# Layer 1 of a two-layer decoder trunk: mean products a step behind their adds, output weights split ahead of convolution taps, a planner that counts more vector work

## The chip, the cores and the metric

The kernel runs on one core of one Trainium2 chip. The metric is the device time of one execution, in microseconds (us). TensorE (PE) multiplies matrices, VectorE (DVE), ScalarE (ACT) and GpSimd (POOL) do elementwise work, and SyncE (SP) issues the transfers. Each engine takes its instructions in the order in which the program lists them for it, and waits at an instruction until what it needs is there.

## The reference

Two residual layers over 2048 tokens of width 1024. Layer 0 (sparse attention beside a gated MLP) is not touched by the change. Layer 1 is a convolution module:

```python
def conv_layer(h, w_in, dw_w, dw_b, ln_g, ln_b, w_out):
    a, gl, z = jnp.split(h @ w_in, 3, axis=-1)
    y = a * jax.nn.sigmoid(gl)
    y = depthwise_causal_conv(y, dw_w, taps=31) + dw_b      # per channel
    y = jax.nn.silu(layer_norm(y, ln_g, ln_b))
    return (y * jax.nn.silu(z)) @ w_out

x = x + rms_norm(conv_layer(rms_norm(x, g_pre), ...), g_post)
```

(`depthwise_causal_conv` stands for the grouped convolution call of the original.)

## The kernel before, in words

Layer 1 works on the sequence in two halves of 1024 tokens. `layer1_in` multiplies the normalised input by the input weights on PE (L161 to L163: every product is three, of high and low parts) and leaves, per 128 channels, a gated tile `y` of 1024 tokens (evicted by DVE at L1007) or a gate `z`, which goes to memory.

The convolution has 31 taps per tile and is shared out by a planner that runs while the program is written. `conv_vector` issues a tap on DVE (L1134, accumulating into `acc`, which lies in PSUM in a pool named `psc` with two slots). `conv_pool` issues a tap as a product on ACT (L1100) and an add on POOL (L1101, into `cacc` in SBUF). DVE joins the two sums in one add (L1140, `cout`), which is stored to `yc_d` in memory. The planner keeps a clock for DVE (`"v"`) and one for POOL (`"p"`); `busy` adds the assumed length of an instruction, and `beat` advances the time by the length of one PE tile (5.12) and issues taps on each of the two until its clock has caught up. So assumed lengths decide how many taps go into the order between other work. `drain(half, k)` issues all taps that are left.

`gated_norm(c, hand)` is a generator of eight steps for a chunk c of 256 tokens (c = 0 to 7; 0 to 3 belong to the first half, 4 to 7 to the second). It loads the convolved chunk from `yc_d`; adds and folds it over channels (L1214, L1202, L1203 on DVE) and takes the mean by a product with a matrix of ones (L1207 on PE); subtracts (L1221), squares on ACT (L1223), adds on POOL (L1224), folds and takes the mean again (L1202, L1203, L1207); square root on ACT (L1233), reciprocal (L1234) and scaling (L1245) on DVE; silu on ACT (L1251), gate on POOL (L1253); and splits the result into high and low parts (L122 on ACT, L125 on POOL). The sum, its folds and the mean product stand in one step. `l(c, m)` advances chunk c to step m.

`wout_pieces` loads the output weights in four pieces of 128 x 4 x 512 into a raw slot and splits each (L122 on ACT, L125 on DVE). `out_project` then makes the output of 128 tokens, called a row tile t0, t1, ... here: 48 matmuls (L842 to L844) in two PSUM tiles, a sum of squares on ACT (L854), square root (L865) and reciprocal (L866), the eviction with the post-norm (L874, `yn`, on DVE), the residual add on POOL (L875) and the store. Chunk c gives t(2c) and t(2c+1).

`tail` holds the order. While the second half's input products run, the norms of c = 0 to 2 are advanced; then the output weights are split; then the loop over c issues the row tiles, with the norms of later chunks and the last taps between them. Before c = 2 the pool `psc` is closed and its PSUM is given to the row tiles, and `gated_norm(4)` starts with `drain(2, 0)`. The Tile framework schedules the written program once more, so the order that stands on each engine is shown below from the built program.

Of the kernel before, what the change touches and what calls it, by code (L numbers as in the profile page):

```python
# [10 lines left out]
F32 = mybir.dt.float32  # L11
# [8 lines left out]
P = 128  # L20
# [61 lines left out]
class Trunk:  # L82
# [723 lines left out]
    def wout_pieces(self, W, raws, places, which, w, lo):  # L806

        nc = self.nc
        w = w if w else {}
        for i in which:  # L810
            n, h = divmod(i, 2)
            w[n, h] = [self.tile(pool, [P, 4, 512], F32R, *tag) for pool, *tag in places[i]]
            pool, tag, *bufs = raws[i]
            raw = self.tile(pool, [P, 4, 512], F32, tag, *bufs)
            nc.sync.dma_start(raw, W[512 * h:512 * h + 512, 512 * n:512 * n + 512]
                              .rearrange("(k p) n -> p k n", p=P))
            self.split(*w[n, h], raw, nc.scalar, lo)
        return w

    def wout_early(self):  # L820
# [257 lines left out]
    def conv_pool(self):  # L1078


        nc = self.nc
        room = lambda c, n: c["end"] - c["tap"] > n
        q = [c for c in self.queue if room(c, 1)]
        if not q:
            q = [c for c in self.now if room(c, 1 if c["sum"] else 6)]
        if not q:
            return False
        c = q[0]
        c["end"] -= 1
        win, w = self.conv_args(c, c["end"])  # L1090
        if c["sum"] is None:
            c["sum"] = self.tile(self.cp, [P, HALF], F32, "cacc", 2)
            if c["bias"] is None:
                nc.scalar.activation(c["sum"], win, AF.Copy, scale=w)
            else:
                nc.scalar.activation(c["sum"], win, AF.Identity, scale=w, bias=c["bias"])
                c["bias"] = None
        else:
            t = self.tile(self.cp, [P, HALF], F32, "prod", 2)
            nc.scalar.activation(t, win, AF.Copy, scale=w)  # L1100
            nc.gpsimd.tensor_tensor(c["sum"], c["sum"], t, ALU.add)  # L1101
            self.busy("p", 2.4)
        return True

    def conv_args(self, c, j):
# [3 lines left out]
    def conv_vector(self):  # L1109

        nc, v = self.nc, self.nc.vector
        if len(self.now) < 2 and self.queue:
            self.now.append(self.queue.pop(0))
        if not self.now:
            return False
        c = self.now.pop(0)
        j = c["tap"]
        c["tap"] += 1
        win, w = self.conv_args(c, j)
        last = c["tap"] == c["end"]  # L1120
        old, acc = c["acc"], c["acc"]
        if last and not (acc and c["sum"]):
            acc = self.tile(self.cp, [P, HALF], F32, "cout", 1)
        elif acc is None:
            acc = self.tile(self.psc, [P, HALF], F32, "acc", 2)
        if old is None and (last or self.clock["p"] < self.clock["v"] + AHEAD):
            old, c["sum"] = c["sum"], None
        if old is None and c["bias"] is not None:
            v.tensor_scalar(acc, win, w, c["bias"], ALU.mult, ALU.add)
            c["bias"] = None  # L1130
        elif old is None:
            v.tensor_scalar(acc, win, w, None, ALU.mult)
        else:
            v.scalar_tensor_tensor(acc, win, w, old, ALU.mult, ALU.add)  # L1134
        c["acc"] = acc
        self.busy("v", 1.2 if self.now else 1.33)
        if last:
            if c["sum"]:
                acc = self.tile(self.cp, [P, HALF], F32, "cout", 1)
                v.tensor_tensor(acc, c["acc"], c["sum"], ALU.add)  # L1140
                self.busy("v", 1.33)
            r, s = P * c["k"], HALF * c["half"]
            nc.sync.dma_start(self.yc_d[r:r + P, s:s + HALF], acc)
        else:
            self.now.append(c)
        return True
# [28 lines left out]
    def gated_norm(self, c, hand):  # L1175

        nc, pool = self.nc, self.lp
        v = nc.vector
        b4 = lambda: self.tile(pool, [P, 4, 256], F32, "b4", 5)
# [25 lines left out]
        def mean(s):  # L1205
            o = self.tile(*self.pt)
            nc.tensor.matmul(o[:, :256], self.mean1, s[:, 0], start=True, stop=True)  # L1207
            return o[:, :256]
# [4 lines left out]
        s = tmp()  # L1213
        v.tensor_tensor(s, Y[0], Y[1], ALU.add)  # L1214
        fold(s)
        m = mean(s)
        self.busy("v", 2.1)
        yield
        sq = []
        for y in Y:  # L1220
            v.tensor_tensor(y, y, wide(m), ALU.subtract)  # L1221
# [4 lines left out]
        self.busy("p", 2.3)  # L1226
        yield
        fold(sq[0])
        var = mean(sq[0])
        self.busy("v", 0.9)  # L1230
        yield
        rs = self.tile(self.late_conv, [P, 256], F32, "lrs", 1)
        nc.scalar.activation(rs, var, AF.Sqrt, bias=self.eps)  # L1233
        v.reciprocal(rs, rs)  # L1234
# [13 lines left out]
        for q, (y, z) in enumerate(zip(Y, zs)):  # L1248
            for i in range(4):
                k = 4 * q + i  # L1250
# [5 lines left out]
        hi, lo = (self.tile(pool, [P, KT, 256], F32R, f"h{2 + 4 * (c % 2) + i}") for i in range(2))  # L1256
        for q, y in enumerate(Y):
            s = slice(4 * q, 4 * q + 4)
# [11 lines left out]
    def tail(self, w1):  # L1270

        with ExitStack() as ctx:
            self.gp = self.pool(ctx, "gpost")
            lp = self.lp = self.pool(ctx, "late")
# [14 lines left out]
            step = lambda g, n=1: [next(g, None) for _ in range(n)]  # L1289
# [14 lines left out]
            n = 8  # L1304
# [4 lines left out]
            def l(c, m):  # L1309
                while c < n and at[c] < m:  # L1310
                    next(ln[c])
                    at[c] += 1
# [4 lines left out]
            for i in range(1, 44):  # L1317
                step(z)
                for c in range(3):
                    l(c, min(7, i + 1 - c))  # L1320
            step(z)
            places = [[(lp, "whiA"), (lp, "wloA")], [(lp, "h0"), (lp, "h1")],
                      [(inner, "whiB"), (inner, "wloB")], [(lp, "h4"), (lp, "h5")]]
            wout = lambda which, w=None: self.wout_pieces(self.a["odd_w_out"][0], [(lp, "wraw")] * 3 + [(lp, "h6")], places, which, w, self.nc.vector)
            w = wout([0])
            step(z, 2)
            w = wout([1], w)
            gpost = self.load_gpost(1)
            l(0, 8)
            step(z, 3)  # L1330
            w = wout([2, 3], w)
            for c in range(n):
                t0, t1 = (self.out2(c, i, hand[c], w, gpost) for i in range(2))
                if c == 2:
                    self.pt = self.ps, [P, 512], F32, "A", 3
                    self.psx.close()
                    self.ps = self.pool(self.psx, "ps4", 4, PSUM)
                step(t0), self.beat()
                l(c + 1, 8), l(c + 2, 2)
                step((t0, t1)[c == 0]), self.beat()  # L1340
                l(c + 2, 3)
                step((t0, t0)[c == 0]), self.beat(5.12 if c == 0 else 0)
                step((t1, t0)[c == 0]), self.beat(5.12 if c else 0)
                l(c + 2, 5)
                step(t1), self.beat()
                l(c + 2, 7), l(c + 3, 1)
                step(t1)


    def run(self):  # L1350
# [60 lines left out]
```

## Time and profile before

| | |
|---|---|
| Time, median of 3 runs | 2279.05 us (2277.89 to 2279.7) |
| Profiled execution, its own time | 2275.86 us, of which span 2274.1 |
| PE busy | 2202.5 us, 97% of the span |
| DVE, ACT, POOL busy | 68%, 55%, 62% |

The profile follows one execution. A row of the stretches view gives, for a window, the busy time and the number of instructions of each engine and the granted clock of PE as a share of full speed (1.00 is 2.4 GHz, 0.50 is 1.2 GHz). A row of the waits view says for which instruction of another engine an engine stood idle, for how long in all, how often, and the longest. A row of the timeline gives start, length, engine, line and operation, and in brackets the idle time before it with what ended it.

### The profile page before, as it was taken

The page shows a single profiled execution, that of the slowest core. Times are in us where ns is not written, and L with a number is a line of the kernel's source. Part 1 is how long each engine was busy: PE and PEld are TensorE (multiplying, and loading weights), DVE is VectorE, ACT ScalarE, POOL GpSimd, SP SyncE. Part 2 cuts the span into 40 slices and gives each one's busy share as a digit, 9 for nine tenths or more (in the row PEclk, how much of TensorE's full clock was granted, in tenths as well). Part 3 has the DMA queues.
Part 4 walks back from the last instruction along what each step waited for, and adds up shares of the span by engine and source line. Part 5 has one row for each costly group of instructions (what it writes and reads, how often), then busy time and mean ns, then how long its engine had stood idle before and what let it go on. Part 6 is the DMA issues. An engine that isn't in the chain of part 4 may idle for free.

```text
span 2274.1 us, 34588 instructions
## 1 busy us (share of the span) xinstructions
PE 2202.5 (97%) x12414; PEld 1907.0 (84%) x12414; DVE 1547.0 (68%) x3272; ACT 1258.6 (55%) x2345; POOL 1400.6 (62%) x1351
## 2 busy tenths in 40 slices
PE   8999999999989999999999989999999989998998
PEld 7898889988878999898998978888888778886877
DVE  3441324365248998888889844527998899999772
ACT  5231232253258888878898854425555575556463
POOL 5232222243237778667789644548999579999683
PEclk9999999999999999999999999999999999999999
DMA  6252231442281111100113154651222432224641
GB/s 161 94 190 88 79 107 53 145 138 86 89 235 53 32 41 29 29 22 25 29 54 110 45 169 151 215 187 47 84 75 83 139 111 65 74 93 145 226 167 65
DMA packets 244860, 229.19 MB, mean 101 GB/s; under 512 B 33841, under 2 KB 206897, under 8 KB 244432
## 3 DMA queue, kind: packets, MB, share of 16 engines
q1 hardware_dynamic: 244688, 226.98, 31.5%
q8 instruction: 98, 1.61, 0.3%
q14 instruction: 74, 0.61, 0.1%
HBM read 157.73 MB, written 69.21 MB: 100 GB/s over the span
## 4 chain that ended last, share of the span: by engine, by line
PE 64%; DVE 15%; POOL 10%; issue 5%; ACT 3%; DMA 2%; SPq 1%; DVEq 0%; POOLq 0%; ACTq 0%
POOL cacc L1101 7%; PE T L708 7%; PE A L161 7%; PE A L162 7%; PE A L163 7%; DVE acc L1134 6%; PE O L731 4%; PE A L576 4%; PE O L730 4%; PE A L577 4%; PE A L844 4%; PE A L843 4%; PE A L842 4%; PE A L173 2%; PE A L175 2%
## 5 line engine op out<-in xcount | busy, mean ns | idle before, releaser
L1134 DVE SCALAR_TENSOR_TENSOR acc<-y,const_taps,acc 128x1024 f32<-128x1024 f32 x304 | 378.9, 1281 | 4.0
L1101 POOL TENSOR_TENSOR cacc<-cacc,prod 128x1024 f32<-128x1024 f32 x145 | 371.7, 2569 | 14.5 <-ACT prod L1100 7.2
L125 POOL TENSOR_TENSOR wlo<-wraw,whi 128x2048 fp32r<-128x2048 f32 (+1 forms) x26 | 120.8, 4647 | 314.8 <-ACT whi L122 279.5
L125 DVE TENSOR_TENSOR ptl<-T,pth 128x512 fp32r<-128x512 f32 (+1 forms) x414 | 263.8, 659 | 20.8 <-ACT pth L122 17.9
L122 ACT CAST pth<-T 128x512 fp32r<-128x512 f32 (+1 forms) x414 | 221.6, 579 | 50.4 <-PE T L708 40.3
L1100 ACT ACTIVATE prod<-y,const_taps 128x1024 f32<-128x1024 f32 x145 | 165.2, 1149 | 139.1 <-POOL cacc L1101 138.9
L161 PE MATMUL A<-hhi,whi 128*128 128x512 f32 x608 | 237.8, 391 | 0.0
L163 PE MATMUL A<-hhi,wlo 128*128 128x512 f32 x608 | 236.8, 389 | 0.0
L162 PE MATMUL A<-hlo,whi 128*128 128x512 f32 x608 | 236.8, 389 | 0.0
L685 POOL TENSOR_SCALAR Ps<-Ps,attn_ssm,gates 128x256 f32<-128x256 f32 (+15 forms) x128 | 161.1, 1259 | 110.9 <-DVE attn_ssm L682 77.9
L730 PE MATMUL O<-pth,V 128*128 128x256 f32 x824 | 220.7, 292 | 0.0
L731 PE MATMUL O<-ptl,V 128*128 128x256 f32 x824 | 219.5, 293 | 1.0 <-POOL ptl L717 0.4
L576 PE MATMUL A<-K,q 128*128 128x320 f32 (+4 forms) x544 | 206.7, 384 | 9.0 <-DVE attn_smx L580 4.4
L577 PE MATMUL A<-K,q 128*128 128x320 f32 (+4 forms) x544 | 183.7, 343 | 0.0
L680 ACT ACTIVATE Ps<-Ps,attn_nm 128x256 f32<-128x256 f32 (+15 forms) x128 | 155.8, 1217 | 31.3 <-DVE attn_nm L678 29.2
L580 DVE CUSTOM_DVE_ANT_1 Ps<-A,attn_bm 128x512 f32<-128x512 f32 (+3 forms) x264 | 154.8, 611 | 22.9 <-PE A L577 11.4
L708 PE MATMUL T<-ident,Ps 128*128 128x128 f32 x1088 | 164.3, 273 | 2.2 <-DVE ptl L125 1.8
L731 PEld LDWEIGHTS O<-ptl,V 128*128 128x128 f32 x824 | 155.6, 189 | 8.5 <-DVE ptl L125 4.2
L730 PEld LDWEIGHTS O<-pth,V 128*128 128x128 f32 x824 | 155.7, 189 | 2.5
L162 PE MATMUL A<-h,whiA 128*128 128x512 f32 x384 | 151.1, 394 | 0.0
L161 PE MATMUL A<-h,whiA 128*128 128x512 f32 x384 | 150.3, 393 | 0.7 <-DVE y L1007 0.7
L161 PE MATMUL A<-h,whiB 128*128 128x512 f32 x384 | 149.7, 390 | 1.2 <-ACT b L1025 1.2
(388 smaller groups left out, 6197.1 us busy)
## 6 DMA issues: line engine op xcount, KB each, us to landing
wraw<-in_even_w_in_dram SPq DMA_DIRECT2D x24, 1024.0 KB, 6.0
q<-q_d SPq DMA_DIRECT2D x128, 128.0 KB, 2.8
wraw<-in_odd_w_in_dram SPq DMA_DIRECT2D x32, 512.0 KB, 4.6
x<-x_d SPq DMA_DIRECT2D x21, 512.0 KB, 3.3
a_d<-osum SPq DMA_DIRECT2D x128, 64.0 KB, 2.1
x<-in_x_dram SPq DMA_DIRECT2D x16, 512.0 KB, 5.6
x_d<-x SPq DMA_DIRECT2D x16, 512.0 KB, 2.6
wraw<-in_odd_w_in_dram SPq DMA_DIRECT2D x8, 1024.0 KB, 4.9
```

Of the source, the lines that this page charges most:

```text
L122: self.nc.scalar.copy(hi, src)
L125: lo_eng.tensor_tensor(lo, src, hi.bitcast(F32), ALU.subtract)
L161: nc.tensor.matmul(o, whi[:, k, wk], hhi[:, k], start=(k == 0), stop=False)
L162: nc.tensor.matmul(o, whi[:, k, wk], hlo[:, k], start=False, stop=False)
L163: nc.tensor.matmul(o, wlo[:, k, wk], hhi[:, k], start=False, stop=(k == KT - 1))
L576: nc.tensor.matmul(out, q[:, 0, r, :], K[:, g, ks], start=True, stop=False)
L577: nc.tensor.matmul(out, q[:, 1, r, :], K[:, g, ks], start=False, stop=True)
L708: nc.tensor.transpose(pt[:, c:c + P], ps[r], self.ident)
L730: nc.tensor.matmul(O, v, hi[:, c], start=(i + j == 0), stop=False)
L731: nc.tensor.matmul(O, v, lo[:, c], start=False, stop=(i + j == len(items) - 1))
L1101: nc.gpsimd.tensor_tensor(c["sum"], c["sum"], t, ALU.add)
L1134: v.scalar_tensor_tensor(acc, win, w, old, ALU.mult, ALU.add)
```

## The change

Four things are edited, and nothing is computed differently. Pieces 1 and 3 of the output weights get raw slots of half a piece in the five-slot buffer `b4` in place of the single slot `wraw` (and `h6`). The planner assumes 2.5 for a POOL add and 1.245 for a DVE tap (2.4 and 1.2 before), and it now counts the splits of the output weights and the evictions of the row tiles. In `gated_norm` the two mean products are issued one step later than the folds that they read. And in `tail` the steps of c = 0 to 2 are spaced more widely (`i - 1 - 3 * c` for `i + 1 - c`), step 8 of c = 1 is written ahead of the loop, and step 4 of c + 2 is issued explicitly. Lines behind line 820 move by 2 in the changed kernel (L1134 to L1136, L1207 to L1209, L842 to L844).

```diff
@@ wout_pieces
             pool, tag, *bufs = raws[i]
-            raw = self.tile(pool, [P, 4, 512], F32, tag, *bufs)
-            nc.sync.dma_start(raw, W[512 * h:512 * h + 512, 512 * n:512 * n + 512]
-                              .rearrange("(k p) n -> p k n", p=P))
-            self.split(*w[n, h], raw, nc.scalar, lo)
+            r = 2 if bufs else 4
+            for k in range(0, 4, r):
+                raw = self.tile(pool, [P, r, 512], F32, tag, *bufs)
+                nc.sync.dma_start(raw, W[512 * h + P * k:512 * h + P * (k + r), 512 * n:512 * n + 512]
+                                  .rearrange("(k p) n -> p k n", p=P))
+                self.split(*(t[:, k:k + r] for t in w[n, h]), raw, nc.scalar, lo)
@@ conv_pool
-            self.busy("p", 2.4)
+            self.busy("p", 2.5)
@@ conv_vector
-        self.busy("v", 1.2 if self.now else 1.33)
+        self.busy("v", 1.245 if self.now else 1.33)
@@ gated_norm
         fold(s)
-        m = mean(s)
         self.busy("v", 2.1)
         yield
+        m = mean(s)
...
         fold(sq[0])
-        var = mean(sq[0])
         self.busy("v", 0.9)
         yield
+        var = mean(sq[0])
@@ tail
-                    l(c, min(7, i + 1 - c))
+                    l(c, min(7, i - 1 - 3 * c))
...
-            wout = lambda which, w=None: self.wout_pieces(self.a["odd_w_out"][0], [(lp, "wraw")] * 3 + [(lp, "h6")], places, which, w, self.nc.vector)
+            def wout(which, w=None):
+                self.busy("v", 3.4 * len(which))
+                return self.wout_pieces(self.a["odd_w_out"][0], [(lp, "wraw"), (lp, "b4", 5)] * 2, places, which, w, self.nc.vector)
...
             w = wout([2, 3], w)
+            l(1, 8)
...
-                step((t0, t0)[c == 0]), self.beat(5.12 if c == 0 else 0)
-                step((t1, t0)[c == 0]), self.beat(5.12 if c else 0)
+                post = lambda t: (step(t), self.busy("v", 1.8), self.busy("p", 2.5))
+                if c:
+                    post(t0)
+                    l(c + 2, 4)
+                    self.beat(0)
+                    step(t1), self.beat()
+                else:
+                    step(t0), self.beat()
+                    post(t0)
+                    l(c + 2, 4)
+                    self.beat()
                 l(c + 2, 5)
                 step(t1), self.beat()
                 l(c + 2, 7), l(c + 3, 1)
-                step(t1)
+                post(t1)
```

The first place is DVE at the norms of c = 0 and 1, before (L214 writes the second half's normalised input; `T` with a number is the mean from PE):

```order
L1214 TENSOR_TENSOR y_20127<-x_20079,x_20080 128x1024
L214 SCALAR_TENSOR_TENSOR h_3894_19732<-acc_20040,const_gpre_87,h_3892_19730 128x512
L1202 TENSOR_TENSOR y_20127<-y_20127 128x512
L214 SCALAR_TENSOR_TENSOR h_3895_19733<-acc_20053,const_gpre_87,h_3893_19731 128x512
L1203 TENSOR_TENSOR y_20127<-y_20127 128x256
L214 SCALAR_TENSOR_TENSOR h_3895_19733<-acc_20066,const_gpre_87,h_3893_19731 128x512
L1221 TENSOR_TENSOR x_20079<-x_20079,T_20131 128x1024
L1221 TENSOR_TENSOR x_20080<-x_20080,T_20131 128x1024
L1214 TENSOR_TENSOR y_20166<-x_20083,x_20084 128x1024
```

and after, at the same place:

```order
L1216 TENSOR_TENSOR y_20177<-x_20077,x_20078 128x1024
L214 SCALAR_TENSOR_TENSOR h_3892_19722<-acc_20060,const_gpre_87,h_3890_19720 128x512
L1204 TENSOR_TENSOR y_20177<-y_20177 128x512
L1205 TENSOR_TENSOR y_20177<-y_20177 128x256
L214 SCALAR_TENSOR_TENSOR h_3892_19722<-acc_20047,const_gpre_87,h_3890_19720 128x512
L214 SCALAR_TENSOR_TENSOR h_3892_19722<-acc_20060,const_gpre_87,h_3890_19720 128x512
L1223 TENSOR_TENSOR x_20077<-x_20077,T_20223 128x1024
L1223 TENSOR_TENSOR x_20078<-x_20078,T_20223 128x1024
L1216 TENSOR_TENSOR y_20310<-x_20081,x_20082 128x1024
```

DVE's own rows are nearly the same; what has moved is the product that makes `T`. Counting PE's matmuls from the first of layer 1, the six mean products of c = 0 to 2 stood at 1298, 1331, 1364, 1398, 1430 and 1489, and stand now at 1335, 1399, 1425, 1524, 1550 and 1652; those of c = 3 and 4 stood at 2528, 2582, 2592 and 2667, and stand at 2532, 2567, 2621 and 2679.

The second place is DVE at the end of the convolution, before (the first two L874 evict t0, the next two t1, the last two t2; the second `cout` row is the layer's last):

```order
L874 SCALAR_TENSOR_TENSOR yn_22106<-A_22010,late_ors_22104,gpost_21923 128x512
L874 SCALAR_TENSOR_TENSOR yn_22106<-A_22076,late_ors_22104,gpost_21923 128x512
L1134 SCALAR_TENSOR_TENSOR acc_21826<-y_21526,const_taps_80,acc_21826 128x1024
L866 RECIPROCAL late_ors_22147<-late_ors_22147 128x1
L1134 SCALAR_TENSOR_TENSOR acc_21826<-y_21526,const_taps_80,acc_21826 128x1024 x3
L1140 TENSOR_TENSOR cout_22042<-acc_21826,cacc_21903 128x1024
L857 TENSOR_SCALAR late_oss_22230<-late_oss_22230 128x1
L874 SCALAR_TENSOR_TENSOR yn_22149<-A_22051,late_ors_22147,gpost_21923 128x512
L874 SCALAR_TENSOR_TENSOR yn_22149<-T_22116,late_ors_22147,gpost_21923 128x512
L866 RECIPROCAL late_ors_22231<-late_ors_22231 128x1
L874 SCALAR_TENSOR_TENSOR yn_22233<-A_22159,late_ors_22231,gpost_21923 128x512
L874 SCALAR_TENSOR_TENSOR yn_22233<-A_22196,late_ors_22231,gpost_21923 128x512
```

and after (here the two L876 evict t3, the folds, L1236 and L1247 belong to the norm of c = 3, and the last row but one is the layer's last `cout`):

```order
L1142 TENSOR_TENSOR cout_22105<-acc_21756,cacc_21924 128x1024
L1136 SCALAR_TENSOR_TENSOR acc_21878<-y_21505,const_taps_80,acc_21878 128x1024
L868 RECIPROCAL late_ors_22337<-late_ors_22337 128x1
L876 SCALAR_TENSOR_TENSOR yn_22339<-A_22256,late_ors_22337,gpost_21890 128x512
L876 SCALAR_TENSOR_TENSOR yn_22339<-A_22286,late_ors_22337,gpost_21890 128x512
L1204 TENSOR_TENSOR b_4213_22233<-b_4213_22233 128x512
L1205 TENSOR_TENSOR b_4213_22233<-b_4213_22233 128x256
L1236 RECIPROCAL lrs_22283<-lrs_22283 128x256
L1247 TENSOR_TENSOR wraw_22143<-wraw_22143,lrs_22283 128x1024 x2
L1142 TENSOR_TENSOR cout_22192<-acc_21878,cacc_21956 128x1024
L1216 TENSOR_TENSOR b_4235_22384<-Y_22331 128x1024
```

The last `cout` has moved from between t0 and t1 to behind the eviction of t3 and behind the reciprocal and scaling of c = 3. Ahead of the eviction of t0 stand 321 of the layer's DVE taps before and 312 now, and one `cout` add fewer.

The third place is PE, where t4 begins (the first row tile of c = 2). Before, its first products (into `A_22342`) stand among those of t2 and t3:

```order
L844 MATMUL A_22196<-h_4181_22004,h_4189_22046 128x512
L842 MATMUL A_22342<-whiA_21830,h_4205_22184 128x512
L843 MATMUL A_22342<-wloA_21831,h_4205_22184 128x512
L844 MATMUL A_22342<-whiA_21830,h_4206_22185 128x512
L842 MATMUL A_22243<-whiA_21830,h_4188_22045 128x512
L843 MATMUL A_22243<-wloA_21831,h_4188_22045 128x512
L1207 MATMUL T_22194<-b_4207_22190,mean_3676_18072 128x256
```

and after, the last products of t3 (into `A_22286`), the variance product of c = 3, and t4 (into `A_22353`):

```order
L845 MATMUL A_22286<-h_4177_21977,h_4180_21986 128x512
L846 MATMUL A_22286<-h_4176_21976,h_4181_21987 128x512
L1209 MATMUL T_22281<-b_4213_22233,mean_3676_18072 128x256
L844 MATMUL A_22353<-whiA_21797,h_4208_22195 128x512
L845 MATMUL A_22353<-wloA_21798,h_4208_22195 128x512
```

In both kernels the first product of t4 waits for the layer's last `cout`, since it writes PSUM that the taps' `acc` held. It was matmul 2518 and is now 2568, directly behind the variance product of c = 3 (2567), which itself stands directly behind the last product of t3 (2566).

## Rows read from the trace of the kernel before

**Rows 1.** Stretches: window, length, busy (count) per engine, clock, DMA share, GB/s.
```profile
1800.00:1900.00 100.00, 93.12 (x409) 75.80 (x408) 93.08 (x71) 64.21 (x81) 68.40 (x24) 0.97 0.34 109
1900.00:2000.00 100.00, 100.00 (x443) 82.82 (x442) 98.98 (x81) 52.03 (x53) 97.70 (x36) 1.00 0.24 79
2050.00:2100.00 50.00, 42.26 (x177) 33.80 (x175) 48.89 (x38) 33.43 (x37) 48.78 (x17) 0.95 0.43 147
```

**Rows 2.** What PE waited for in layer 1: total us, times, longest.
```profile
PE A L1207 <- DVE late_ors L866: 5.4, 2, 4.1
PE A L842 <- DVE yn L874: 4.9, 1, 4.9
PE T L1207 <- DVE y L1203: 4.3, 1, 4.3
PE A L843 <- DVE h L125: 2.3, 1, 2.3
PE T L1207 <- DVE Y L1221: 1.8, 1, 1.8
PE A L843 <- DVE wloB L125: 1.4, 1, 1.4
PE A L161 <- ACT b L1025: 1.2, 1, 1.2
PE A L212 <- DVE h L214: 1.2, 1, 1.2
PE A L212 <- ACT b L1025: 1.1, 1, 1.1
...
PE acc L212 <- DVE cout L1140: 0.4, 1, 0.4
```

**Rows 3.** Stretches of PE at half clock, and from t2's first product on.
```profile
2100.86:2125.30 24.44, 24.44 (x98) 20.00 (x99) 15.32 (x20) 4.49 (x9) 16.68 (x8) 0.91 0.84 284
...
1863.20:1869.60 6.40, 4.73 (x11) 3.85 (x12) 6.40 (x6) 2.52 (x5) 1.60 (x2) 0.50 0.15 46
2194.20:2197.40 3.20, 3.01 (x7) 2.48 (x8) 2.86 (x6) 1.76 (x2) 1.49 (x1) 0.50 0.40 164
```

**Rows 4.** Timeline of DVE at the end of the convolution and behind it.
```profile
2099.98 1.39 DVE L874 SCALAR_TENSOR_TENSOR yn<-A,late_ors,gpost 128x512 f32<-128x512 f32 x2
...
2106.82 1.23 DVE L1140 TENSOR_TENSOR cout<-acc,cacc 128x1024 f32<-128x1024 f32 x1 [0.27 <-DMA yc_d<-cout]
...
2122.25 1.59 DVE L1214 TENSOR_TENSOR b<-Y 128x1024 f32<-128x1024 f32 x1 [3.05 <-DMA Y<-yc_d]
```

**Rows 5.** The page's group of all DVE taps: busy, mean ns, idle before.
```profile
L1134 DVE SCALAR_TENSOR_TENSOR acc<-y,const_taps,acc 128x1024 f32<-128x1024 f32 x304 | 378.9, 1281 | 4.0
```

**Rows 6.** Timeline of PE: last product of t3, and the variance product of c = 3.
```profile
2126.67 0.39 PE L844 MATMUL A<-h,h 128*128 128x512 f32 x1
...
2128.71 0.59 PE L1207 MATMUL T<-b,mean 128*128 128x256 f32 x2
```

**Rows 7.** Timeline of DVE behind them.
```profile
2128.14 0.17 DVE L866 RECIPROCAL late_ors<-late_ors 128x1 f32<-128x1 f32 x1 [2.05 <-ACT late_ors L865]
2128.34 1.41 DVE L874 SCALAR_TENSOR_TENSOR yn<-A,late_ors,gpost 128x512 f32<-128x512 f32 x2
2129.85 1.75 DVE L1234 RECIPROCAL lrs<-lrs 128x256 f32<-128x256 f32 x1
2131.64 2.86 DVE L1245 TENSOR_TENSOR wraw<-wraw,lrs 128x1024 f32<-128x1024 f32 x2
```

**Rows 8.** Timeline of DVE: adds and folds of the norms of c = 0 to 2.
```profile
1823.83 0.41 DVE L1203 TENSOR_TENSOR y<-y 128x256 f32<-128x256 f32 x1
...
1830.38 2.77 DVE L1202 TENSOR_TENSOR y<-y 128x512 f32<-128x512 f32 x1
1833.19 2.50 DVE L1203 TENSOR_TENSOR y<-y 128x256 f32<-128x256 f32 x1
```

**Rows 9.** Timeline of POOL beside the second and third of these.
```profile
1829.21 3.40 POOL L1224 TENSOR_TENSOR y<-y,y 128x1024 f32<-128x1024 f32 x1
1832.57 8.18 POOL L1101 TENSOR_TENSOR cacc<-cacc,prod 128x1024 f32<-128x1024 f32 x3
```

**Rows 10.** Timeline of SP: the last convolved tile to memory, and back.
```profile
2110.80 0.38 SPq L1143 DMA_DIRECT2D yc_d<-cout  x1
...
2113.38 0.45 SPq L1198 DMA_DIRECT2D Y<-yc_d  x1
```

## The prediction

> **What bounds the kernel now.** I read the table of stretches first, then the list of what PE waits for, then the timelines of DVE, POOL and SP around the longest waits. PE is busy 97% of the span, so only two things can be won in layer 1: time in which PE stands idle, and time at half clock. The table shows where: PE is idle 6.9 of 100 us at the norms of c = 0 to 2, none of the 100 us behind, and 7.7 of 50 us where the output weights come in [rows 1]. By the list of waits, layer 1 idles 3.9 us for the transposes of the second half (1.2, 1.2, 1.1, 0.4), 6.1 us for the norms of c = 0 to 2 (4.3 and 1.8), 3.7 us for the split output weights (2.3 and 1.4), 4.9 us for the eviction of t0, which frees the PSUM of t2, and 5.4 us for two means among the last row tiles (booked to DVE's late_ors) [rows 2]. That is 24 us, 1.1% of the time, and each longer stop is followed by a stretch at half clock [rows 3].
>
> The second thing to see is that DVE is nearly as full as PE. From 1900 to 2000 us it works 98.98 of 100 us, and from 2050 to 2100 us 48.89 of 50 [rows 1]. In that stretch a DVE result comes as early as the work listed ahead of it allows, and PE's waits there are waits for DVE's list. So for each result I count what stands ahead of it.
>
> **The change, part by part.** The same matmuls, splits, evictions and norms are done, 324 DVE taps for 325 and 146 POOL adds for 145. So no work goes; what counts is the order.
>
> *The spread mean products and the half slots.* Ahead of the first product of t2, PE can win the transposes (3.9), the norms (6.1, and 2.4 of half clock, since 4.73 busy us were spent at 0.50 [rows 3]) and the output weights (3.7). The weights' waits should go whole, because 9 to 12 fewer taps (12 to 16 us) stand ahead of their splits and DVE was late by 2.3 at most. Of the other 12.4 I take half: DVE's list at the transposes is shorter by some 8 us, but the mean products of c = 0 to 2 wait no less for DVE's folds, which now have taps between them. That makes 6.2 + 3.7 = 9.9 (3.7 to 16). If nothing of it came, PE would be back to its old arrival.
>
> *The eviction of t0.* DVE's tap costs 1.281 [rows 5] and a cout add 1.23 [rows 4]; nine taps and one such add fewer stand ahead of it: 9 x 1.281 + 1.23 = 12.8 us. Its first half ended at 2099.98 + 0.70 = 2100.7 [rows 4], so now at 2087.9. Against it stands the stage of c = 0 to 2: the mean of c = 0 stands 37 matmuls later, 8.4 us at 443 matmuls in 100 us [rows 1], and DVE waits for it at its subtraction with all later work behind. Before, DVE idled 6.9 us in that stretch [rows 1]; how much of one replaces the other no row shows. Bounds: 5 us won (most of the idle time back) to 5 us lost (the 8.4 less a part covered by evictions); I take 1.5 lost, near the middle, a little on the side of the new wait. So the eviction frees PSUM at 2089.4. PE, which came at 2095.9 and now comes 9.9 earlier, at 2086.0, still waits 3.4. t2 starts at 2089.4 in place of 2100.9, a gain of 11.5 us, and it is DVE that sets it.
>
> *The last cout.* This is what the change gives back. From t2's first product to that of t4 are 98 matmuls, which took 24.4 us with the half clock in them [rows 3], so t3 ends near 2113.7. Now t4 waits for the last cout, and DVE comes to that add only behind the eviction of t3, the folds and the reciprocal and scaling of c = 3, with PE's variance product between. From the rows: last product of t3 to the reciprocal of its norm 2128.14 - 2126.67 = 1.5 [rows 6, 7]; reciprocal and eviction 1.6 [rows 7]; two folds, 1.1 if they run like the 0.41 [rows 8], 5.3 if like the 2.77 and 2.50 beside POOL [rows 8, 9], and POOL then has the residual add of t3 and a last product, so I take 3.9; product to reciprocal 2129.85 - 2128.71 = 1.1 [rows 6, 7]; reciprocal 1.75 and scaling 2.86 [rows 7]; the cout 1.23. Sum 14 (11 to 18, the top with the scaling slowed too). PE stands still all that time, since t4 is the next thing on its list. Before, the last cout ended at 2108.05 [rows 4], before PE needed it. So t4's first product comes at 2113.7 + 14 = 2127.7; before, the same count of matmuls was reached at 2125.3 [rows 3]. All 11.5 us are gone, and 2.4 us more.
>
> *Behind it.* A stop of that length is followed by some 3.2 us at half clock, as at 2194.2 [rows 3]: 1.6 us. The norm of c = 4 needs the last cout back from memory: before, from its end to the add on DVE 2122.25 - 2108.05 = 14.2 us [rows 4], of which 2.75 until the store was issued [rows 10], which now has nothing ahead of it; 11.5 and two folds, about 13.5 to 14, stand against 53 matmuls (12.0 and the half clock), so 0.5 late (0 to 5). In the last row tiles 5.4 us of waits and 1.5 us of half clock go [rows 2, 3]; but the products of c = 4 to 7 still wait for chains through DVE, ACT and POOL with 58 to 106 matmuls to cover them, and I put 4.5 (0 to 10) in their place: -2.4.
>
> Sum: 2.4 + 1.6 + 0.5 - 2.4 = +2.1 us on the profiled execution's own 2275.86. That one lies 3.2 us below the median of its three runs, 2279.05; put on the median, it makes about **2281 us**, no change that counts. What a measurement of this kernel can tell from no change is 0.2%, 4.6 us.
>
> **A rule weighed.** The same fold takes 0.41 us alone and 2.50 us while POOL adds [rows 8, 9]. The Trainium skill (GPSIMD Engine Reference, 1. Specifications) says that the two engines share their SBUF access, with contention for DVE instructions of two SBUF inputs; the fold is such a one, and the trace agrees. By that rule the order change is bad for folds, for they now stand between products. It is the slower rival below, with prices from the rows.
>
> **The rivals.** *Folds at POOL's pace, slower.* The place is the eviction of t3 to the last cout, and the folds of c = 0 to 2. There POOL has products or the residual add at hand all the time, and every add and fold goes like the 2.50 to 2.77. Then the stop before t4 is 18 (4 more), DVE loses 5 instead of 1.5 in the norms (3.5 more), and the folds of c = 4 are late too (2 more): 2.1 + 9.5 = 11.6, about 2290.5. It decides from 2.5 us over my sum. For it: POOL is 97.70% busy from 1900 us on [rows 1]. Against it: POOL was only 68.40% busy in the norms' stretch, and it idles once the products end. Chance of slower by over 0.2%: 0.36.
>
> *The early gains last, faster.* DVE gets 5 us of its idle time back (6.5 better than my value), the folds before the last cout run alone (2.8 better), the tail waits 2.5 in place of 4.5: 2.1 - 11.3 = -9, about 2270. For it: PE's list gives each norm step twice the room. Against it: 14 us between t3 and t4 are a chain of which 10 us are there even without any sharing. Chance of faster by over 0.2%: 0.26.
>
> *The change does not do what it says.* The products stand later but PE still waits for folds that stand later too; only the weights' 3.7 and half of the transposes come. PE then reaches t2 at 2090.2, 0.8 later than DVE frees it: 2.9, about 2282. It lies within my own case, since DVE and not PE sets the start of t2.
>
> **How the numbers follow.** Within 0.2%: 0.38, the likeliest case, with its own range of 2275 to 2284. For 8 times in 10 the range takes in most of both rivals: from 2268 to 2294. It adds the bounds of the norms' stage (-6.5 to 3.5), of the stop (-3 to 4), of the reload (0 to 4.5) and of the tail (-4.5 to 5.5), not all at one end.
>
> **What would show it.** In the changed profile: PE's waits for the transposed halves, wloB and h are short or gone; the one long wait of PE is at L844 for cout, 11 to 18 us, in front of t4, with a half-clock stretch behind it; t2 starts some 11 us earlier than before, and t4 within 4 us of before. The sum is wrong if PE does not stop in front of t4, which would mean that DVE reached the last cout early; if the list of waits puts more than 6 us at the products L1209; or if DVE shows idle time of over 5 us while c = 0 and 1 are normed, which would move t2.

## The result, and the profile after

The changed kernel takes 2304.52 us (median of 4 runs, 2300.88 to 2305.4) against 2279.38 us (2277.89 to 2280.61): ratio 1.0112, 95% interval 1.01 to 1.0125. It is slower by 25 us where 2281 was predicted, outside the range. The profiled execution took 2300.88 us, its span 2299.2, 25.1 more than before.

The 25.1 us split at two marks. Layer 1's first product (L161) comes at 1519.81, 0.2 earlier. t2's first product comes at 2113.04 in place of 2100.86: +12.2 (predicted -11.5). From there to the product 98 matmuls later, which begins t4 in the changed kernel, pass 39.3 us in place of 24.4: +14.9 (predicted +13.9). From that product to the end pass 146.8 in place of 148.8: -2.0 (predicted -0.3). So nearly the whole error, 23.7 us, lies ahead of t2.

PE's longest waits in layer 1, in the list of waits after (columns as in [rows 2]):

```profile
PE A L844 <- DVE yn L876: 8.9, 1, 8.9
PE T L1209 <- DVE b L1205: 6.9, 1, 6.9
PE A L844 <- DVE cout L1142: 6.0, 1, 6.0
PE A L845 <- DVE wloB L125: 5.2, 1, 5.2
PE A L161 <- ACT b L1027: 5.0, 1, 5.0
PE T L1209 <- DVE y L1205: 3.4, 2, 2.7
PE T L1209 <- ACT lrs L1235: 2.2, 1, 2.2
PE A L845 <- DVE h L125: 2.2, 2, 1.7
PE A L161 <- DVE y L1009: 2.1, 1, 2.1
PE A L1209 <- DVE late_ors L868: 1.9, 1, 1.9
```

The wait for t0's eviction has grown from 4.9 to 8.9 [rows 2], though PE came to it 8.2 later, at 2113.04 - 8.93 = 2104.11 against 2095.94. Ahead of it the transposed half cost more (5.0 and 2.1 at L161), and so did the output weights (5.2 for `wloB`, 1.4 before). Only the mean among the last row tiles is better, 1.9 for 5.4.

The stop in front of t4 came as predicted, in two pieces. The first rows are PE's timeline, the second DVE's beside it:

```profile
2145.22 1.19 PE L1209 MATMUL T<-b,mean 128*128 128x256 f32 x2 [6.88 <-DVE b L1205]
2152.38 0.77 PE L844 MATMUL A<-whiA,h 128*128 128x512 f32 x1 [5.97 <-DVE cout L1142]
```

```profile
2140.58 1.41 DVE L876 SCALAR_TENSOR_TENSOR yn<-A,late_ors,gpost 128x512 f32<-128x512 f32 x2
2141.91 0.68 DVE L1204 TENSOR_TENSOR b<-b 128x512 f32<-128x512 f32 x1
2142.62 2.44 DVE L1205 TENSOR_TENSOR b<-b 128x256 f32<-128x256 f32 x1
2146.95 1.75 DVE L1236 RECIPROCAL lrs<-lrs 128x256 f32<-128x256 f32 x1 [1.88 <-ACT lrs L1235]
2148.74 2.36 DVE L1247 TENSOR_TENSOR wraw<-wraw,lrs 128x1024 f32<-128x1024 f32 x2
2151.02 1.22 DVE L1142 TENSOR_TENSOR cout<-acc,cacc 128x1024 f32<-128x1024 f32 x1
```

PE stands for 6.88 + 5.97 = 12.85 us while DVE goes through eviction, folds, reciprocal, scaling and `cout`: 14 (11 to 18) was predicted. The two folds took 3.1 (3.9 predicted), the scaling 2.36 (2.86).

What went wrong stands in the stretches. The first row is before, the others are after (columns as in [rows 1]):

```profile
1600.00:1700.00 100.00, 100.00 (x442) 82.80 (x442) 97.89 (x81) 58.85 (x60) 96.85 (x38) 1.00 0.23 78
```

```profile
1600.00:1700.00 100.00, 100.00 (x442) 82.81 (x442) 81.58 (x67) 50.75 (x53) 83.00 (x32) 1.00 0.23 79
1800.00:1900.00 100.00, 94.32 (x420) 76.67 (x421) 89.26 (x78) 56.74 (x69) 66.54 (x25) 0.98 0.36 116
1900.00:2000.00 100.00, 100.00 (x443) 82.81 (x442) 89.08 (x71) 55.15 (x60) 90.09 (x33) 1.00 0.21 69
2050.00:2100.00 50.00, 42.62 (x179) 34.18 (x178) 48.32 (x32) 30.25 (x32) 49.19 (x17) 0.97 0.55 188
```

Beside the first half's input products, where PE runs without a gap, DVE works 81.58 of 100 us in place of 97.89 and POOL 83.00 in place of 96.85; from 1900 on DVE works 89.08 in place of 98.98 [rows 1]. What DVE waited for from 1536 us to the eviction of t0, first before, then after:

```profile
DVE acc L1134 <- POOL cacc L1101: 11.4, 4, 5.3
DVE y L1007 <- PE A L163: 11.0, 3, 5.2
DVE h L214 <- ACT h L213: 4.5, 3, 2.7
```

```profile
DVE acc L1136 <- POOL cacc L1103: 21.0, 5, 8.3
DVE y L1009 <- PE A L163: 19.1, 5, 5.1
DVE h L214 <- ACT h L213: 9.9, 4, 4.9
```

These three rows grow by 9.6, 8.1 and 5.4 us, 23.1 together: DVE waits for POOL's sum where a tap starts from it, and for PE's products and ACT's transposed tiles where no tap stands ahead.

The idle time is not spread evenly. Of the 18.4 us that DVE idles from 1600 to 1700, three waits behind one finished tile make 16.3, in DVE's timeline after:

```profile
1645.21 0.69 DVE L1009 SCALAR_TENSOR_TENSOR y<-b,A 128x512 f32<-128x512 f32 x1 [3.37 <-PE A L163]
1650.65 0.69 DVE L1009 SCALAR_TENSOR_TENSOR y<-b,A 128x512 f32<-128x512 f32 x1 [4.75 <-PE A L163]
1659.47 3.42 DVE L1136 SCALAR_TENSOR_TENSOR acc<-y,const_taps,cacc 128x1024 f32<-128x1024 f32 x1 [8.13 <-POOL cacc L1103]
```

DVE has 67 instructions there in place of 81, 17% fewer, for an assumed length that is 4% longer. Why the planner's order changes so much more than in proportion is not shown.

### The profile page after: what moved, and what is told of

It is laid out like the page before. It is cut to its first block, busy times and chain, and to the rows that moved or that the text cites. A ratio compares the mean times of both kernels' runs of the same rounds, so it can differ in the third digit from the quotient of the medians.

```text
span 2299.2 us, 34591 instructions
## 1 busy us (share of the span) xinstructions
PE 2207.8 (96%) x12414; PEld 1909.7 (83%) x12414; DVE 1546.6 (67%) x3274; ACT 1260.5 (55%) x2348; POOL 1400.1 (61%) x1352
## 4 chain that ended last, share of the span: by engine, by line
PE 73%; DVE 13%; POOL 5%; issue 4%; ACT 3%; DMA 2%; SPq 1%; DVEq 0%; POOLq 0%; ACTq 0%
PE A L161 9%; PE A L162 9%; PE A L163 9%; PE T L708 7%; DVE acc L1136 6%; PE A L846 4%; PE A L844 4%; PE A L845 4%; PE O L731 4%; PE A L576 4%; PE O L730 4%; PE A L577 4%; POOL cacc L1103 3%; PE A L173 2%; PE A L177 2%
## 5 line engine op out<-in xcount | busy, mean ns | idle before, releaser
L1136 DVE SCALAR_TENSOR_TENSOR acc<-y,const_taps,acc 128x1024 f32<-128x1024 f32 x304 | 382.5, 1283 | 4.8
L161 PE MATMUL A<-hhi,whi 128*128 128x512 f32 x608 | 237.8, 391 | 0.0
L161 PE MATMUL A<-h,whiB 128*128 128x512 f32 x384 | 151.5, 395 | 5.0 <-ACT b L1027 5.0
L161 PE MATMUL A<-h,whiA 128*128 128x512 f32 x384 | 149.2, 391 | 2.8 <-DVE y L1009 2.1
L163 PE MATMUL A<-h,wloB 128*128 128x512 f32 x384 | 150.9, 393 | 0.0
```

The costliest lines, as they stand in the source:

```text
L161: nc.tensor.matmul(o, whi[:, k, wk], hhi[:, k], start=(k == 0), stop=False)
L163: nc.tensor.matmul(o, wlo[:, k, wk], hhi[:, k], start=False, stop=(k == KT - 1))
```

## The experiments

My theory from the two traces: the planner's longer lengths leave DVE and POOL without taps beside the input products, and what is not done there delays t0's eviction and the last `cout`. Its rivals: the order of `tail` does it, by its spacing or by the `cout` behind c = 3; the half slots do it, by their splits; and, later, the long length costs only by the taps that start from POOL's sum and wait for it.

The table gives for each kernel the time's ratio to the kernel before, and from the trace, in us from layer 1's first product: DVE's work and idle time up to the end of the first half of t0's eviction, that end (their sum), the end of the last `cout`, and the end of PE's last product. Taps are DVE's, ahead of that eviction.

| kernel | ratio (95%) | taps | work | idle | t0 evicted | last cout | PE ends |
|---|---|---|---|---|---|---|---|
| before | 1 | 321 | 537.0 | 43.6 | 580.7 | 588.0 | 748.0 |
| after | 1.0112 (1.0100-1.0125) | 312 | 528.4 | 64.7 | 593.2 | 632.4 | 773.4 |
| e1 | 1.0055 (1.004-1.007) | 313 | 531.3 | 51.9 | 583.2 | 619.6 | 761.0 |
| e2 | 1.0085 (1.007-1.01) | 321 | 542.9 | 57.7 | 600.6 | 612.5 | 768.4 |
| e3 | 0.9984 (0.9974-0.9994) | 321 | 536.8 | 44.5 | 581.3 | 588.6 | 744.3 |
| e4 | 1.0023 (1.0013-1.0032) | 321 | 544.7 | 45.4 | 590.0 | 597.2 | 758.1 |
| e5 | 1.0246 (1.0229-1.0263) | 290 | 510.1 | 93.3 | 603.4 | 665.2 | 805.7 |
| e6 | 1.0008 (0.9999-1.0017) | 326 | 540.9 | 43.2 | 584.1 | 591.2 | 752.4 |
| e7 | 1.0091 (1.0076-1.0106) | 316 | 539.5 | 52.0 | 591.5 | 613.3 | 770.2 |
| e8 | 1.0024 (1.0014-1.0034) | 322 | 540.4 | 48.5 | 588.9 | 596.4 | 756.1 |
| e9 | 1.0083 (1.0062-1.0103) | 320 | 544.7 | 45.8 | 590.4 | 612.1 | 768.2 |
| e10 | 1.0012 (1.0001-1.0022) | 320 | 528.2 | 48.5 | 576.7 | 614.2 | 750.1 |
| e11 | 1.0105 (1.009-1.012) | 303 | 515.8 | 63.2 | 579.0 | 628.4 | 769.8 |
| e12 | 1.0096 (1.0081-1.0112) | 316 | 539.3 | 50.3 | 589.6 | 611.6 | 768.5 |
| e13 | 1.0156 (1.0136-1.0176) | 325 | 520.6 | 60.0 | 580.7 | 648.0 | 784.2 |
| e14 | 1.0139 (1.012-1.0158) | 331 | 523.5 | 56.9 | 580.4 | 638.3 | 779.9 |
| e15 | 1.0152 (1.0135-1.0169) | 330 | 523.2 | 59.8 | 582.9 | 644.0 | 785.3 |
| e16 | 1.0271 (1.0254-1.0287) | 327 | 530.4 | 78.8 | 609.2 | 670.2 | 810.0 |

### The assumed lengths

**e1**, the changed kernel with the old lengths:

```diff
-            self.busy("p", 2.5)
+            self.busy("p", 2.4)
-        self.busy("v", 1.245 if self.now else 1.33)
+        self.busy("v", 1.2 if self.now else 1.33)
```

> The changed kernel with the assumed lengths of a tap set back to 1.2 (DVE) and 2.4 (POOL); all else as changed. Theory 1 (the longer assumed lengths make the planner issue too few taps beside the input products, so DVE and POOL stand idle there and the convolution ends late): the 25 us go, 2268 to 2284 us, and DVE idles under 5 of the 100 us from 1600 to 1700 us, where the changed kernel idles 18. Theory 2 (the output stage's new order, with the last cout behind the eviction of t3, costs the time): 2295 us or more, since that order stays.

2289.67 us, between the two ranges: by the ratios (1.0055 and 1.0112) about half of the loss goes. DVE's idle time falls by 12.8 us, and beside the first half's products DVE is full again, in the stretches of e1:

```profile
1600.00:1700.00 100.00, 100.00 (x443) 82.82 (x442) 97.94 (x81) 58.19 (x60) 96.81 (x37) 1.00 0.22 74
```

Counted from the layer's first product, t2 begins 2.4 us later than before in e1 and 12.4 later in the changed kernel. The stop in front of t4 stays: from t2 to t4's first product pass 36.5 us (39.3 in the changed kernel, 24.4 before), with this row in PE's timeline of e1:

```profile
2140.94 0.77 PE L844 MATMUL A<-whiA,h 128*128 128x512 f32 x1 [9.03 <-DVE cout L1142]
```

So in this pair the lengths make 10 of the 12.4 us lost ahead of t2, and the late last `cout` is what remains.

**e2**, the reverse: the kernel before with 2.5 and 1.245.

> The kernel before with the assumed lengths of the changed one (1.245 and 2.5) and nothing else. Theory 1: 2293 to 2308 us, with DVE idle over 10 of the 100 us from 1600 to 1700 us. Theory 2: 2275 to 2284 us.

2296.89 us, in the range of theory 1. The two lengths alone cost 0.85%; DVE works 81.66 of the 100 us from 1600 on, as in the changed kernel.

**e5** and **e6** split e2: 1.245 alone, and 2.5 alone, each in the kernel before.

> The kernel before with the DVE tap's assumed length 1.245 for 1.2 and nothing else. If both lengths act alike (each leaves its own engine idle beside the input products): 2284 to 2292 us. If the DVE tap alone makes the 20 us of both: 2293 to 2300 us. If POOL alone does: within 4 us of before.

> The kernel before with the POOL add's assumed length 2.5 for 2.4 and nothing else. If both lengths act alike: 2283 to 2291 us. If the DVE tap alone makes the 20 us: within 4 us of before. If POOL alone does: 2293 to 2300 us.

2333.11 us, far above every range, and 2278.7. It is DVE's length; POOL's alone changes nothing that counts. DVE's waits in e5 up to t0's eviction:

```profile
DVE y L1007 <- PE A L163: 39.9, 7, 17.5
DVE acc L1134 <- POOL cacc L1101: 29.1, 7, 11.0
```

31 taps fewer stand ahead of t0's eviction, 26.9 us less work, and yet it comes 22.7 later, since DVE idles 49.7 more. This is the plainest case against counting the list alone. The last `cout` of the first half's convolution ends 277.3 us after the layer's first product in the kernel before, in e1, e3 and e12, and 293.9, 294.1 and 297.5 after it in the changed kernel, e2 and e5. With 2.5 added, 1.245 costs 19 us (e2) in place of 56 (e5), so the two lengths cannot be valued apart.

**e9**, the changed kernel with 1.2 for DVE and 2.5 for POOL.

> The changed kernel with the DVE tap's assumed length alone set back to 1.2 (POOL stays at 2.5). If the DVE tap's length is what leaves DVE idle beside the input products of the first half: 2286 to 2295 us, as with both set back, and DVE idle under 6 of the 100 us from 1600 to 1700 us. If the two lengths only count together: 2299 to 2306 us.

2295.56 us, 0.6 above the first range, and DVE idles 1.2 of the 100 us. Eight taps and 16.2 us of work come back ahead of t0's eviction, 19.0 us of idle time goes, and the eviction comes 2.7 earlier, the last `cout` 20.4 earlier. So in the changed kernel the taps that no longer stood ahead had been exchanged for idle time.

### The other parts

**e3**, the kernel before with the mean products a step late:

```diff
         fold(s)
-        m = mean(s)
         self.busy("v", 2.1)
         yield
+        m = mean(s)
```

and the same for `var`.

> The kernel before with the two mean products of each norm issued a step behind their folds and nothing else. Theory 1: 2272 to 2284 us, and PE's waits at the mean products (11.5 us before) are halved. A third theory (DVE waits for the later products and loses what PE gains): 2288 us or more.

2273.64 us, below both kernels, and faster than the one before by 0.06 to 0.26%. PE's waits at the mean products fall from 11.5 to 8.8 us, less than I expected. Up to the last `cout` nothing moves by more than 0.7 us; the gain is in the last row tiles, where the wait of 5.4 us [rows 2] is down, in the list of PE's waits of e3:

```profile
PE A L1207 <- DVE late_ors L866: 2.2, 2, 1.6
```

**e4**, the kernel before with the half slots for the weights' pieces 1 and 3 (the first hunk of the diff, and the slots):

```diff
-            wout = lambda which, w=None: self.wout_pieces(..., [(lp, "wraw")] * 3 + [(lp, "h6")], places, which, w, self.nc.vector)
+            wout = lambda which, w=None: self.wout_pieces(..., [(lp, "wraw"), (lp, "b4", 5)] * 2, places, which, w, self.nc.vector)
```

> The kernel before with the half-piece raw slots for the output weights and nothing else. Theory 1: 2273 to 2281 us; the 3.7 us that PE waits for split weights go or shrink. Theory 2 says nothing on it.

2281.71 us, just above the range and by the ratio 5 us slower than the kernel before. DVE does the same 321 taps but 7.7 us more work. Two splits of e4 in DVE's timeline:

```profile
2081.06 2.21 DVE L125 TENSOR_TENSOR h<-b,h 128x1024 fp32r<-128x1024 f32 x1
...
2085.58 4.40 DVE L125 TENSOR_TENSOR wloB<-wraw,whiB 128x2048 fp32r<-128x2048 f32 x1
```

In the kernel before, this split of `wloB` took 2.28 us; the two that are now halves took 3.31 and 2.28 whole, and take four times 2.2. PE's waits for split weights grow in place of going: 4.2 for `wloB` (1.4 before) and 3.4 for `h` (2.3).

**e8**, e3 with the counts (3.4 per piece of weights, 1.8 and 2.5 per row tile), and **e7**, e3 with the new order in `tail` without counts, lengths and half slots:

```diff
+                self.busy("v", 3.4 * len(which))
+                post = lambda t: (step(t), self.busy("v", 1.8), self.busy("p", 2.5))
```

```diff
-                    l(c, min(7, i + 1 - c))
+                    l(c, min(7, i - 1 - 3 * c))
+            l(1, 8)
+                    post(t0)
+                    l(c + 2, 4)
```

> The kernel before with the late mean products and the splits and evictions of the output stage counted in the planner's clocks, without the half slots, the longer lengths and the tail's new order. Theory A: 2270 to 2278 us, no wait for cout over 2 us. Theory B: 2281 to 2290 us, with a wait of PE for cout of over 5 us in front of t4.

> The kernel before with the late mean products and the tail's new order (spaced steps of c = 0 to 2, step 8 of c = 1 ahead of the loop, step 4 of c + 2 issued explicitly), without the half slots, the longer lengths and the newly counted work. Theory A (the order puts the last cout behind the eviction of t3): 2281 to 2290 us, with a wait of PE for cout of over 5 us in front of t4. Theory B (it is the counted splits and evictions that push taps behind): 2270 to 2278 us, without that wait.

2282.34 and 2297.9 us. Neither theory fits: e8 has the time of theory B and e7 is slower than both ranges, but the wait for `cout` that went with the slower range appears in neither. What has grown is PE's wait for the eviction of t0, from 4.9 us in e3 to 12.5 in e8 and 12.9 in e7. **e12** has only the spaced steps, the first two lines of that diff:

> The kernel before with the late mean products and the wider spacing of the steps of c = 0 to 2, and nothing else of the tail's new order. If the spacing is what costs in that order: 2284 to 2298 us, with the eviction of t0 over 6 us later from the layer's start than before and PE's waits at the means of c = 0 to 2 no shorter. If it is the later edits of the loop: 2270 to 2278 us.

2298.7 us, 0.7 above the first range and as e7: the spacing alone makes the cost of the order. The eviction of t0 comes 8.9 us later than before. PE's longest waits in e12:

```profile
PE A L842 <- DVE yn L874: 17.1, 3, 12.8
PE A L1207 <- DVE late_ors L866: 9.9, 1, 9.9
PE T L1207 <- DVE y L1203: 6.5, 3, 2.6
PE A L843 <- DVE wloB L125: 6.3, 1, 6.3
```

All of PE's waits in layer 1 are 44.7 us in e12 and 23.5 in e3; PE's end is 24.2 later. The norms of c = 0 to 2 gain nothing by the wider spacing (6.5 and 0.8 for ACT, against 4.8 and 1.8 in e3), and the three waits that grow, from 4.9 to 17.1, from 2.2 to 9.9 and from 1.6 to 6.3, are all for DVE behind them, at the weights and the row tiles.

### The start from POOL's sum

`conv_vector` lets a tile's first tap on DVE start from `cacc` when POOL's clock is less than `AHEAD` (8.0) in front of DVE's; such a tap waits for POOL. A rival held that the long length costs by these waits alone. **e10** is e3 with `AHEAD = 4.0`, **e11** e3 with 1.17 for 1.2:

```diff
-AHEAD = 8.0
+AHEAD = 4.0
```

```diff
-        self.busy("v", 1.2 if self.now else 1.33)
+        self.busy("v", 1.17 if self.now else 1.33)
```

> The kernel before with the late mean products and with AHEAD, which decides whether DVE starts a tile from POOL's sum, 4.0 for 8.0. If DVE's waits for POOL's sums (11.4 us before) are time that the end of the convolution gets back: they shrink to under 5 us and the time is 2266 to 2272 us. If the taps that are then placed elsewhere cost as much: 2272 to 2282 us.

> The kernel before with the late mean products and the DVE tap's assumed length 1.17 for 1.2. If the longer length costs because DVE is left idle, a shorter one has little to win, since DVE is 98% busy there: 2269 to 2280 us. If any other length upsets the order as much as 1.245 did: over 2285 us.

2279.39 and 2300.26 us. In e10 DVE's waits for POOL's sums shrink to 4.9 us and t0's eviction comes 4.6 us earlier than in e3, but the last `cout` 25.6 later, and the time is worse by 6. In e11 a shorter length too costs 1%, as the second range had it; t0's eviction comes 2.3 us earlier than in e3, but the last `cout` 39.8 later, and PE stops 18.4 us for it. DVE's waits in e11:

```profile
DVE acc L1134 <- POOL cacc L1101: 32.0, 6, 16.4
DVE y L1007 <- PE A L163: 11.9, 4, 5.2
```

Four runs forbid the start from the sum altogether: **e13** in the changed kernel, **e14** in e3, **e15** and **e16** in e3 with 1.17 and 1.245.

```diff
-AHEAD = 8.0
+AHEAD = -1e9
```

> The changed kernel with AHEAD at -1e9: DVE never starts a tile's taps from POOL's sum but joins it at the end with a cout add. If DVE's early waits for POOL's sums are the idle time that the change brought: the 21 us of them go, 2283 to 2296 us. If too few taps beside the input products are: DVE still idles over 12 of the 100 us from 1600 to 1700 us, 2298 us or more.

> The kernel before with the late mean products and AHEAD at -1e9. 11.4 us of waits for POOL's sums go, a few cout adds of 1.2 us come: 2268 to 2278 us by either theory.

> As the last, with the DVE tap assumed at 1.17. If the start from POOL's sum is the cause of the 23 us that 1.17 cost: 2268 to 2282 us, within 8 us of the run with 1.2. If not: over 2288 us.

> As the one with 1.2, with the DVE tap assumed at 1.245. If the start from POOL's sum is the cause of the 56 us that 1.245 cost: 2270 to 2290 us. If too few taps beside the input products are: 2300 us or more, with DVE idle over 12 of the 100 us from 1600 to 1700 us.

2312.97, 2310.56, 2311.97 and 2339.66 us. e14 is far above its range. e13 and e16 have the times that I gave for too few taps, but not the idle time that went with them: DVE idles 3.2 and 9.6 of the 100 us, not over 12. e15 lies above 2288, but so does the run with 1.2 that it was to be measured by. Without such starts the last `cout` moves to 638 us and more, and PE stops for it, in e13:

```profile
PE A L844 <- DVE cout L1142: 31.7, 1, 31.7
```

What can be compared are e14 to e16 among themselves. 1.17 and 1.2 come out alike, which speaks for the waits for POOL's sum as the price of 1.17 in e11; it is not shown, since without such starts all taps stand elsewhere. 1.245 stays 29 us slower with no such wait, so these waits are not the whole price of the long length. DVE's waits in e16:

```profile
DVE h L214 <- ACT h L213: 27.4, 10, 7.5
DVE y L1007 <- PE A L163: 20.5, 9, 5.2
```

DVE stands at transposed tiles and at products with no tap listed ahead of them. The first half's convolution ends at 300.7 us from the layer's start in e16, at 285.0 in e14 and 279.4 in e15. From e14 to e16 this delay grows, to 28.8 us at t0's eviction and 30.1 at PE's end; e15's lead over e14 is gone by t0's eviction.

## Why the prediction was wrong

**The step that failed: the eviction of t0.** It took DVE's list as the only thing that sets this result ("a DVE result comes as early as the work listed ahead of it allows"), so a list shorter by 12.8 us was an eviction earlier by 11.5. Its time is work plus idle time, and idle time was held to the 6.9 us of one stage, with bounds of 5 us. In fact the work fell by 8.6 us and the idle time grew by 21.1, from 43.6 to 64.7. e1 removes 12.8 of these by the lengths alone; e9 trades 19.0 of them for 16.2 of work. I treated the lengths as something that only moves taps behind the eviction. They also set how many taps stand beside PE's input products, 67 instructions in place of 81 from 1600 on, where DVE has nothing else to do; a tap that is missing there is not saved but left for later.

**The 8.6 itself** is the sum of larger parts, from DVE's rows of that stretch in both kernels: taps -7.0 (11.5 predicted), the additions and folds of `y` 22.1 for 28.2, so -6.1, the splits of `h` and of the weights +4.7, the rest -0.2. The missing `cout` add was none: 10 stand there in both; one of the nine taps was a last one that writes `cout` itself.

**The spread mean products and half slots.** PE was to come 9.9 us earlier (3.7 to 16) and came 8.2 later. The waits around the transposes cost 8.3 us in place of 4.0, with a new stretch at half clock (4.63 busy us at 0.50 from 1777.6 to 1784.4) around the longest, the weights 7.4 in place of 3.7, and the norms' stage 5.7 in place of 6.8. That the weights' waits go "whole", because fewer taps stand ahead, fails for the reason e4 shows: the halves and `wloB` are split beside POOL's work at twice the price. I had weighed that sharing for folds only. e12 shows the spaced steps to be a loss by themselves.

At the transposes I counted DVE's list alone. The longest wait there, 5.03 us up to 1779.77, is for ACT, which stood at a product of the convolution that waited for POOL, just ahead of the eviction (L1027) that PE needed, in ACT's timeline after:

```profile
1778.08 1.15 ACT L1102 ACTIVATE prod<-y,const_taps 128x1024 f32<-128x1024 f32 x1 [4.06 <-POOL cacc L1103]
```

**The last cout** was right in place and size: 12.85 us for 14, and 39.3 us from t2 to t4 for 38.4. **Behind it** -2.0 for -0.3. The half clock behind the stop is as I had it, 3.22 us at 0.50 from 2152.38 on. The last `cout` comes back from memory sooner than I had it, 6.6 us from its end to the add on DVE (11.5 taken), in DVE's timeline after, which answers to the third of [rows 4]:

```profile
2158.81 1.50 DVE L1216 TENSOR_TENSOR b<-Y 128x1024 f32<-128x1024 f32 x1 [6.58 <-DMA Y<-yc_d]
```

And of the 5.4 us of means in the last row tiles 1.9 are left; e3 shows that the late products alone do that.

**The rivals.** The slower one named the folds at the stop and in the norms; at the stop they took 3.1 us, less than I had, and the adds and folds of `y` 6.1 less than before, so the kernel is slower for another reason. Of the signs that I had named against my sum, DVE idle for over 5 us in the norms' stage showed (10.7 from 1800 to 1900). L1209 has 14.4 us, over the 6 that I named, but 6.9 of them are the stop itself.

**What stays open.** The parts do not add up: by the ratios late means give -4 us (e3), half slots +5 (e4), counts +9 (e8 against e3), spacing +26 (e12 against e3), lengths +19 (e2); their sum, 55, is over twice the 25 that were measured. With the old lengths, all the other parts together cost 12.5 us (e1), less than the spacing alone (e12). Each edit lets the planner place all later taps anew, and no run isolates one displaced tap. Nor does a run show which edit puts the last `cout` behind t3: PE has no stop for it in front of t4 in e2, e4, e7, e8, e9 and e12. It is shown that the late eviction of t0, by DVE's idle time, and the late last `cout` carry the loss, and that setting the lengths back takes away about half of it, most of that ahead of t2 (e1); why the order with all parts comes out better than that with the spacing alone is not settled.

## What to carry to other kernels

When an engine is nearly full, date its result by work plus idle time from a fixed start, and look at what an edit does to the idle time of the stages before, not only at how many instructions stand ahead. Taps that a planner withholds from a stretch in which another engine sets the pace come back later, where the next stage waits. Try each constant of such a planner by itself: here the late mean products alone are the edit worth keeping, 0.16% faster than the kernel before.

## What the runs showed of the hardware that was not expected

A tap that starts from POOL's sum reads two operands from SBUF and costs, in the mean, twice and more what a tap on the PSUM sum does. The page's groups of DVE after:

```profile
L1136 DVE SCALAR_TENSOR_TENSOR acc<-y,const_taps,acc 128x1024 f32<-128x1024 f32 x304 | 382.5, 1283 | 4.8
...
L1136 DVE SCALAR_TENSOR_TENSOR acc<-y,const_taps,cacc 128x1024 f32<-128x1024 f32 x14 | 40.3, 2880 | 21.0 <-POOL cacc L1103 21.0
```

1.28 against 2.88 us. The price goes with POOL's work: three of the 14 ran while POOL stood idle, at 1597.58, 1750.58 and 1938.15, and took 1.29 us each; the other eleven took 2.2 to 5.5. The first of the three on DVE, and POOL's next instruction with its idle time:

```profile
1597.58 1.29 DVE L1136 SCALAR_TENSOR_TENSOR acc<-y,const_taps,cacc 128x1024 f32<-128x1024 f32 x1
1600.13 4.88 POOL L1103 TENSOR_TENSOR cacc<-cacc,prod 128x1024 f32<-128x1024 f32 x2 [3.59 <-ACT cacc L1096]
```

Of the four half-piece splits of 1024 columns one took 1.21 us and the others 2.2 to 2.35. Two of them in DVE's timeline after, and the POOL add that started with the first:

```profile
2074.80 1.21 DVE L125 TENSOR_TENSOR h<-b,h 128x1024 fp32r<-128x1024 f32 x1
2077.12 2.21 DVE L125 TENSOR_TENSOR h<-b,h 128x1024 fp32r<-128x1024 f32 x1
```

```profile
2074.81 3.45 POOL L1103 TENSOR_TENSOR cacc<-cacc,prod 128x1024 f32<-128x1024 f32 x1
```

The split of 1.21 us began 0.01 us ahead of that add, and the add took 3.45, where adds beside taps on the PSUM sum take 2.4; the split of 2.21 began while the add ran. In these rows the one that starts second pays. That is also how `wloB` took 2.28 in the kernel before and 4.40 in e4: in the first it began 0.54 us ahead of a POOL add, which took 4.00, in the second 0.09 us behind one.

Taps from POOL's sum and splits both have two SBUF inputs. The Trainium skill (GPSIMD Engine Reference, 1. Specifications) has DVE instructions of that kind contend with POOL for SBUF; the taps agree, 1.28 us with one such input and 2.88 with two. And a tap of 1.28 us does not take 1.28 of the list: two in a row take 2.46, so they stand 1.18 apart:

```profile
2113.56 2.46 DVE L1136 SCALAR_TENSOR_TENSOR acc<-y,const_taps,acc 128x1024 f32<-128x1024 f32 x2
```

The old 1.2 lies nearer to that than 1.245, and the 1.281 with which I priced nine fewer taps was too much.
